# The first tap of the convolutions on ScalarE, and the low parts of their weights on VectorE instead of GpSimd

## The chip, the core and the metric

The kernel runs on one core of a Trainium2 chip. The core has a matrix engine (TensorE, PE in the profile), an elementwise engine (VectorE, DVE), an engine for activation functions and scaled copies (ScalarE, ACT), a general engine (GpSimd, POOL) and SyncE (SP), which here only issues DMAs. Each engine takes its own instructions strictly in order, and waits on semaphores for the others. The metric is the device time of one execution in microseconds; lower is better.

## The reference, cut to what matters

The reference is one step of a small diffusion backbone with 128 context and 512 latent tokens of width 1024: a mixer (neighbourhood attention and a gated DeltaNet in both directions) followed by an MLP. All of it is in float32. The part around the change projects the normalised tokens to the 1536 DeltaNet channels, convolves every channel along the tokens with five taps (context and latent tokens apart, each with zero padding), and applies silu:

```python
p = h @ w_in
dn_qkv = jax.nn.silu(_dwconv(dn_qkv, conv_w))      # CONV_W = 5, one filter per channel
dq, dk, dv = jnp.split(dn_qkv, [DN_QK_WIDTH, 2 * DN_QK_WIDTH], axis=-1)
dq = _l2n(dq.reshape(B, T, DN_HEADS, DN_DK))
dk = _l2n(dk.reshape(B, T, DN_HEADS, DN_DK))
```

What follows the projection (the DeltaNet, the attention, the merge and the MLP) takes most of the time and is not touched.

## The kernel before

TensorE multiplies float32 numbers as two rounded parts. Every operand is split into a high part (a cast to the rounded type) and a low part (the operand minus its high part), and a product is three matmuls: high with high, high with low, low with high. The helper `split` (lines 176 to 184) does it for a weight block of 128 x 1024 numbers: ScalarE makes the high part at line 182, and the engine named by `eng` makes the low part at line 183. `load_w` is a load through SyncE (line 174) and a split. The low part is formed by VectorE unless the call says otherwise; the call for the convolution's blocks says GpSimd. Four buffers each hold high and low parts.

The tokens (640 columns) stay in `hhi` and `hlo`, made in a front stage in which TensorE, VectorE, ScalarE and SyncE follow an order written out by hand. There VectorE forms a scaled copy `hf` (line 382) and the low part of one slice of the tokens (line 385) for TensorE's products at line 391; first VectorE has to form the modulation factors (line 247 and 250) from which ScalarE makes the high part.

Then come the twelve weight blocks of the DeltaNet channels, in three groups of four (q, k, v). For each block TensorE makes two products of 320 columns into two of two PSUM banks (lines 202 to 204, 48 matmuls). ScalarE copies them into a padded row buffer `cvb` (lines 624, 625, 626; there are two such buffers), which frees the banks. The five taps are one scaled copy and four multiply-adds on 128 x 644 numbers, all on VectorE:

```python
y = cb.tile([P, 644], F32, tag="y", name="y", bufs=2)
V.tensor_scalar(y, b[:, 0:644], cw[:, mt * 5 : mt * 5 + 1], None, op0=ALU.mult)   # line 628
for j in range(1, 5):
    V.scalar_tensor_tensor(y, b[:, j : j + 644], cw[:, mt * 5 + j : mt * 5 + j + 1], y,
                           op0=ALU.mult, op1=ALU.add)                             # line 630
```

Silu is a tanh on ScalarE (line 633) and a multiply-add on VectorE (line 634), which writes the block's channels. In the q group ScalarE also squares them (line 637) and TensorE sums the squares (line 639). In the k and v groups TensorE transposes the finished channels (line 643) once per block; ScalarE copies and squares the k results (lines 651, 653) and VectorE scales the v results (line 647), which are stored through ScalarE's DMA queue.

Beside the blocks run small chains: the z products (ScalarE 502, VectorE 503, GpSimd 504 and a store), the decay rates (VectorE 532 to 552, ending in `gg`, which TensorE reads at line 558), the norms of q and k (VectorE 149 to 158) and some factors that GpSimd forms and index rows that it loads (lines 662 to 680, 768, 769). The first weight blocks of the stage behind are cast by ScalarE at line 1055 and get their low parts from VectorE at line 1059.

Outside the hand-ordered stages a planner sets each engine's order before the run. It plays the program with its own costs and lets an engine take the ready instruction that stands first in the program. So the order around the twelve blocks is the planner's, and it follows which engine each instruction is given to. The front stage before and the stages behind the first two units of the next projection are ordered by hand.

Of the kernel before, what the change touches and what calls it, by code (L numbers as in the profile page):

```python
# [13 lines left out]
AF = mybir.ActivationFunctionType  # L14
ALU = mybir.AluOpType
# [5 lines left out]
KT = 8  # L21
# [76 lines left out]
def body(ctx: ExitStack, tc: tile.TileContext, I, O, dbg=None):  # L98
    nc = tc.nc
    dbg = dbg or {}  # L100
    V, S, G, PE = nc.vector, nc.scalar, nc.gpsimd, nc.tensor
# [9 lines left out]
    def ps_mm():  # L111
        return pp.tile([P, 512], F32, tag="mm", name="ps_mm", bufs=2)
# [4 lines left out]
    def ps_tb():  # L117
        return pp.tile([P, 512], F32, tag="tb", name="ps_tb", bufs=1)
# [3 lines left out]
    def ps_t3():  # L122
        tcnt[0] += 1
        return ps_tp() if tcnt[0] % 3 else ps_tb()

    def ps_st(i):
        return pp.tile([P, 512], F32, tag=f"st{i}", name=f"ps_st{i}", bufs=1)
# [18 lines left out]
    def newton_rsqrt(pool, x, n, tag, w=None, post=1.0, between=()):  # L146

        y, t, i = [pool.tile([P, w or n], ty, tag=tag + a, name=tag + a)[:, :n] for a, ty in (("y", F32), ("t", F32), ("i", I32))]
        V.tensor_scalar(i, x.bitcast(I32), 1, None, op0=ALU.logical_shift_right)
        V.tensor_scalar(y.bitcast(I32), i, -1.0, float(0x5F3759DF), op0=ALU.mult, op1=ALU.add)  # L150
        for it in range(3):
            V.scalar_tensor_tensor(t, y, -0.5, y, op0=ALU.mult, op1=ALU.mult)
            V.tensor_tensor(t, t, x, op=ALU.mult)
            if it < len(between):
                between[it]()
            V.scalar_tensor_tensor(y, t, 1.5, y, op0=ALU.add, op1=ALU.mult)
        if post != 1.0:
            V.tensor_scalar(y, y, post, None, op0=ALU.mult)
        return y
# [6 lines left out]
    def load_raw(src, pool=None, tag="raw"):  # L166
        if raw3[0] and tag == "raw":
            raw3[1] += 1
            if raw3[1] % 3 == 0:
                pool, tag = (raw3[0], 1), "raw3"  # L170
        pool = pool or (rawp if tag == "raw" else (wpool, 4))
        raw = pool[0].tile([P, 1024], F32, tag=tag, name="raw", bufs=pool[1])
        with tc.issue_after(behind[0]) if behind else ExitStack():
            lastd[0] = nc.sync.dma_start(raw, src).ins
        return raw

    def split(raw, kt, n, pool=None, eng=V):

        pool = pool or wpool
        hi = pool.tile([P, 1024], F32R, tag="whi", name="whi")  # L180
        lo = pool.tile([P, 1024], F32R, tag="wlo", name="wlo")
        S.copy(hi, raw)  # L182
        eng.tensor_tensor(lo, raw, hi.bitcast(F32), op=ALU.subtract)  # L183
        return [x.rearrange("p (k n) -> p k n", k=kt) for x in (hi, lo)]

    def load_w(src, kt, n, pool=None, eng=V):
        return split(load_raw(src), kt, n, pool, eng)
# [10 lines left out]
    def mm3(out, pairs):  # L198

        n = len(pairs)  # L200
        for i, (ah, al, bh, bl) in enumerate(pairs):
            PE.matmul(out, ah, bh, start=(i == 0), stop=False)  # L202
            PE.matmul(out, ah, bl, start=False, stop=False)  # L203
            PE.matmul(out, al, bh, start=False, stop=(i == n - 1))  # L204
# [97 lines left out]
    cw = cv.tile([P, 60], F32, tag="cw", name="cw")  # L302
# [186 lines left out]
    def feat_pairs(whi, wlo, half):  # L489
        a, w = HALVES[half]  # L490
        return [(whi[:, k], wlo[:, k], hhi[:, k, a : a + w], hlo[:, k, a : a + w]) for k in range(KT)]
# [122 lines left out]
    for x in range(3):  # L614
        sT = (kqS[:, 1], kqS[:, 0], vT)[x]
        pss = ps_tb() if x == 0 else None
        for hp in range(HP):
            mt = 4 * x + hp
            whi, wlo = load_w(I["w_dn"][mt], KT, 128, eng=G)
            ps0, ps1 = ps_mm(), ps_mm()  # L620
            mm3(ps0[:, :320], feat_pairs(whi, wlo, 0))
            mm3(ps1[:, :320], feat_pairs(whi, wlo, 1))
            b = cvb[mt % 2]
            S.copy(b[:, 2:130], ps0[:, 0:128])
            S.copy(b[:, 134:326], ps0[:, 128:320])
            S.copy(b[:, 326:646], ps1[:, :320])  # L626
            y = cb.tile([P, 644], F32, tag="y", name="y", bufs=2)
            V.tensor_scalar(y, b[:, 0:644], cw[:, mt * 5 : mt * 5 + 1], None, op0=ALU.mult)
            for j in range(1, 5):
                V.scalar_tensor_tensor(y, b[:, j : j + 644], cw[:, mt * 5 + j : mt * 5 + j + 1], y,  # L630
                                       op0=ALU.mult, op1=ALU.add)
            ty = cb.tile([P, 644], F32, tag="ty", name="ty", bufs=1)
            S.activation(ty, y, AF.Tanh, scale=0.5)
            V.scalar_tensor_tensor(sT[:, hp], ty, 1.0, y, op0=ALU.add, op1=ALU.mult)
            if x == 0:
                s2 = cb.tile([P, 644], F32, tag="s2", name="s2", bufs=2)
                S.activation(s2, sT[:, hp], AF.Square)
                for t in range(5):
                    PE.matmul(pss[:, 8 * t + 2 * hp : 8 * t + 2 * hp + 2], s2[:, TS[t] : TS[t] + 128], halves2, start=True, stop=True)
        for t in range(5) if x else ():  # L640
            ps = ps_t3() if x == 1 else ps_st(t % 3)
            for hp in range(HP):
                PE.transpose(ps[:, hp * 128 : hp * 128 + 128], sT[:, hp, TS[t] : TS[t] + 128], ident)
            if x == 2:
                for d in range(2):
                    vs = cb.tile([P, 644], F32, tag=("s2", "y")[d], name="vs", bufs=2)[:, :512]
                    V.tensor_tensor(vs.rearrange("p (h d) -> p h d", h=8), ps.rearrange("p (h d) -> p h d", h=8),
                                    vsc[:, d, t].unsqueeze(2).to_broadcast([P, 8, 64]), op=ALU.mult)
                    nc.scalar.dma_start(vs_d[d, t], vs)
            else:  # L650
                S.copy(kt[:, t], ps)
                s2 = cb.tile([P, 644], F32, tag="s2", name="s2", bufs=2)[:, :512]
                S.activation(s2, ps, AF.Square)
                V.tensor_reduce(ss[:, t], s2.rearrange("p (h d) -> p h d", h=8), axis=AX.X, op=ALU.add)
        if x < 2:

            s4 = cb.tile([P, 40], F32, tag="s4", name="s4")
            V.tensor_scalar(s4, ss.rearrange("p t h -> p (t h)") if x else pss[:, :40], 4 * EPS, None, op0=ALU.add)
            rs = newton_rsqrt(cb, s4, 40, "l2", post=(0.0625 if x == 0 else 1.0)).rearrange("p (t h) -> p t h", t=5)
            if x == 0:  # L660
                for y in (SF, SB):
                    G.tensor_copy(y[:, :, 4], rs)
                continue

            bb = bp.rearrange("p t (e h) -> p e t h", e=2)
            for d in range(2):
                G.tensor_tensor(bb[:, d], beta[:, :, 8 * d : 8 * d + 8], rs, op=ALU.mult)

            V.tensor_scalar(vsc[:, 1], bb[:, 1], 0.5, None, op0=ALU.mult)
            V.scalar_tensor_tensor(vsc[:, 0], s4.rearrange("p (t h) -> p t h", t=5), 0.5, rs, op0=ALU.mult, op1=ALU.mult)  # L670
            for d in range(2):
                G.tensor_tensor(bb[:, d], bb[:, d], rs, op=ALU.mult)
            G.tensor_copy(SF[:, :, 0], bb[:, 0])
            G.tensor_tensor(SF[:, :, 1], bb[:, 0], E4[:, 1], op=ALU.mult)
            G.tensor_tensor(SB[:, :, 2], bb[:, 1], E4[:, 2], op=ALU.mult)
            for par in range(2):
                sl = slice(64 * par, 64 * par + 64)
                G.tensor_copy(SX[sl, par : par + 9 : 2], SF[sl])
                G.tensor_copy(SX[sl, 1 - par], SB[sl, 0])
                G.tensor_copy(SX[sl, 3 - par : 10 - par : 2][:, ::-1], SB[sl, 1:5])  # L680

            V.scalar_tensor_tensor(rq2, SX[:, :, 4], 4.0 / 64, SX[:, :, 4], op0=ALU.mult, op1=ALU.mult)
# [666 lines left out]
    with (  # L1349
# [161 lines left out]
        with tc.manual_schedule(engines={E_.PE, E_.DVE, E_.Activation, E_.SP}):  # L1511
            late[0] = 1
            rot, oraw, subs = rotations(1, xq), [], []
            for j in range(-2, n + 1):
                hp, b = BLK[min(j + 2, n - 1)]
# [77 lines left out]
    for c in range(4):  # L1593
        whi, wlo = wbr[c]
# [429 lines left out]
    with tc.tile_pool(name="fin", bufs=2, side="right", reuse_waits="tile") as fin_:  # L2024
        gB2 = gate_bcast(1, fin_)
        w = {(kh, nh): split(w2_raw(7, kh, nh), 2, 512) for nh in range(2) for kh in range(2)}
        for blk in (None, (0, 0), (1, 0), (0, 1), (1, 1)):
            r = 0 if blk is None else 1
            if blk is None:
                parts = [(slice(0, 128), 0, slice(0, 128))]  # L2030
                y = [R[4][:, n] for n in range(2)]
                lhs = [[x[:, k] for x in fpr] for k in range(4)]
            else:
                th, pair = blk
                parts = [(slice(64 * j, 64 * j + 64), 1 + 2 * pair + j, slice(64 * th, 64 * th + 64)) for j in range(2)]
                y = [R[2 * th + n][:, pair] for n in range(2)]
# [122 lines left out]
```

## Time and profile before

| | |
|---|---|
| median of 3 runs | 1105.38 us (1104.59 to 1108.61) |
| the profiled execution | 1109.01 us, its span 1107.2 us |
| mean granted TensorE clock of the profiled execution | 0.99 |
| busy share of the span: PE, DVE, ACT, POOL | 96%, 77%, 47%, 28% |
| stretch of the twelve blocks | about 70 to 187 us of the span |

Rows of the timeline give the start and the length in microseconds, the engine, the line, the operation, what it writes and reads, and in brackets how long the engine stood idle before and who ended that. Rows of groups give the count, the busy time, the mean of one in ns, and the idle time before. Rows of waits give the total, the number of waits and the longest. A window's row gives, for each engine, busy time and instructions, and then the granted clock of TensorE as a share of full speed, the DMA engines' busy share and GB/s.

### The profile page before, as it was taken

The page shows a single profiled execution, that of the slowest core. Times are in us where ns is not written, and L with a number is a line of the kernel's source. Part 1 is how long each engine was busy: PE and PEld are TensorE (multiplying, and loading weights), DVE is VectorE, ACT ScalarE, POOL GpSimd, SP SyncE. Part 2 cuts the span into 40 slices and gives each one's busy share as a digit, 9 for nine tenths or more (in the row PEclk, how much of TensorE's full clock was granted, in tenths as well). Part 3 has the DMA queues.
Part 4 walks back from the last instruction along what each step waited for, and adds up shares of the span by engine and source line. Part 5 has one row for each costly group of instructions (what it writes and reads, how often), then busy time and mean ns, then how long its engine had stood idle before and what let it go on. Part 6 is the DMA issues. An engine that isn't in the chain of part 4 may idle for free.

```text
span 1107.2 us, 25427 instructions
## 1 busy us (share of the span) xinstructions
PE 1058.1 (96%) x10323; PEld 945.8 (85%) x10323; DVE 847.4 (77%) x1645; ACT 520.7 (47%) x1142; POOL 308.6 (28%) x276
## 2 busy tenths in 40 slices
PE   6999999999998998999999999999999999999996
PEld 5778989988888897888888999988888979797975
DVE  5557888497687677576857676999798887979775
ACT  5535443434353643336764442765444444444432
POOL 0242312000000001202504235335344352535213
PEclk9999999989999999999999999999999999999999
DMA  9832113564665655657537542465656556545605
GB/s 340 293 124 62 27 32 106 188 233 167 184 189 169 206 169 175 170 157 228 164 95 261 203 165 97 94 173 152 156 150 167 170 140 167 151 135 152 191 20 152
DMA packets 71972, 176.43 MB, mean 159 GB/s; under 512 B 18936, under 2 KB 28408, under 8 KB 71856
## 3 DMA queue, kind: packets, MB, share of 16 engines
q1 hardware_dynamic: 55504, 135.40, 36.5%
q0 software_dynamic: 9808, 24.80, 11.0%
q10 hardware_dynamic: 6544, 14.61, 4.0%
q8 instruction: 81, 1.33, 0.5%
q14 instruction: 35, 0.29, 0.1%
HBM read 150.62 MB, written 24.12 MB: 158 GB/s over the span
## 4 chain that ended last, share of the span: by engine, by line
PE 71%; DVE 19%; ACT 3%; issue 3%; DMA 2%; POOL 0%; DVEq 0%; ACTq 0%
PE ps_mm L1116 6%; PE ps_mm L1118 5%; PE ps_mm L1117 5%; DVE wlo L183 4%; PE ps_mm L1759 3%; PE ps_mm L1758 3%; PE ps_mm L1757 3%; PE ps_mm L202 3%; PE ps_mm L203 2%; PE ps_mm L204 2%; DVE R L1870 2%; DVE y L630 2%; PE ps_st L1759 2%; PE ps_st L1758 2%; PE ps_st L1757 2%
## 5 line engine op out<-in xcount | busy, mean ns | idle before, releaser
L1116 PE MATMUL ps_mm<-hhi,whi 128*128 128x320 f32 x384 | 130.3, 339 | 0.9 <-ACT gth L1072 0.9
L1118 PE MATMUL ps_mm<-hhi,wlo 128*128 128x320 f32 x384 | 120.6, 314 | 1.5 <-issue 1.5
L1117 PE MATMUL ps_mm<-hlo,whi 128*128 128x320 f32 x384 | 120.4, 314 | 0.0
L183 DVE TENSOR_TENSOR wlo<-raw,whi 128x1024 fp32r<-128x1024 f32 x59 | 81.3, 1386 | 21.5 <-ACT whi L182 21.2
L182 ACT CAST whi<-raw 128x1024 fp32r<-128x1024 f32 x78 | 81.0, 1046 | 31.1 <-PE ps_mm L1758 8.5
L1116 PEld LDWEIGHTS ps_mm<-hhi,whi 128*128 128x128 f32 x384 | 74.0, 193 | 10.2 <-issue 6.2
L1117 PEld LDWEIGHTS ps_mm<-hlo,whi 128*128 128x128 f32 x384 | 74.3, 194 | 0.2
L1118 PEld LDWEIGHTS ps_mm<-hhi,wlo 128*128 128x128 f32 x384 | 74.0, 193 | 0.0
L183 POOL TENSOR_TENSOR wlo<-raw,whi 128x1024 fp32r<-128x1024 f32 x19 | 46.5, 2449 | 72.4 <-ACT whi L182 72.4
L202 PE MATMUL ps_mm<-hhi,whi 128*128 128x320 f32 x192 | 60.8, 317 | 1.5 <-ACT cvb L626 1.5
L203 PE MATMUL ps_mm<-hlo,whi 128*128 128x320 f32 x192 | 60.6, 315 | 0.0
L204 PE MATMUL ps_mm<-hhi,wlo 128*128 128x320 f32 x192 | 60.1, 313 | 0.0
L183 DVE TENSOR_TENSOR wlo<-S,whi 128x1024 fp32r<-128x1024 f32 x28 | 54.8, 1973 | 4.2 <-ACT whi L182 4.2
L1359 POOL DMA_DIRECT2D vw<-v_d x32 | 21.1, 674 | 130.3 <-ACT arow L1133 93.2
L183 DVE TENSOR_TENSOR wlo<-T,whi 128x1024 fp32r<-128x1024 f32 x28 | 44.0, 1570 | 15.3 <-ACT whi L182 15.3
L768 POOL DMA_DIRECT2D rls<-ai_d x10 | 5.1, 509 | 174.7 <-PE ps_tb L731 161.8
L1059 DVE TENSOR_TENSOR wlo<-raw,whi 128x1024 fp32r<-128x1024 f32 x35 | 42.7, 1223 | 12.5 <-ACT whi L1055 12.1
L182 ACT CAST whi<-T 128x1024 fp32r<-128x1024 f32 x28 | 29.4, 1050 | 34.2 <-PE ps_mm L1758 16.5
L630 DVE SCALAR_TENSOR_TENSOR y<-cvb,cw,y 128x644 f32<-128x644 f32 x48 | 42.6, 888 | 0.9
L182 ACT CAST whi<-S 128x1024 fp32r<-128x1024 f32 x28 | 28.8, 1051 | 23.9 <-PE ps_tb L204 12.3
L1055 ACT CAST whi<-raw 128x1024 fp32r<-128x1024 f32 x35 | 36.5, 1047 | 7.0 <-issue 6.1
L1072 ACT ACTIVATE gth<-ps_mm 128x320 f32<-128x320 f32 x32 | 14.0, 437 | 53.5 <-PE ps_mm L1131 30.3
(579 smaller groups left out, 3549.1 us busy)
## 6 DMA issues: line engine op xcount, KB each, us to landing
raw<-in_w_ff_dram SPq DMA_DIRECT2D x57, 512.0 KB
raw<-in_w_ada_dram SPq DMA_DIRECT2D x48, 512.0 KB
raw<-in_w_gate_dram SPq DMA_DIRECT2D x16, 512.0 KB
S<-in_w_ff_dram SPq DMA_DIRECT2D x14, 512.0 KB
T<-in_w_ff_dram SPq DMA_DIRECT2D x14, 512.0 KB
S<-in_w_ff_dram POOLq DMA_DIRECT2D x14, 512.0 KB, 5.4
T<-in_w_ff_dram POOLq DMA_DIRECT2D x14, 512.0 KB, 7.1
raw<-in_w_dn_dram SPq DMA_DIRECT2D x12, 512.0 KB
```

Source lines behind the costliest of these rows:

```text
L182: S.copy(hi, raw)
L183: eng.tensor_tensor(lo, raw, hi.bitcast(F32), op=ALU.subtract)
L202: PE.matmul(out, ah, bh, start=(i == 0), stop=False)
L203: PE.matmul(out, ah, bl, start=False, stop=False)
L204: PE.matmul(out, al, bh, start=False, stop=(i == n - 1))
L630: V.scalar_tensor_tensor(y, b[:, j : j + 644], cw[:, mt * 5 + j : mt * 5 + j + 1], y, op0=ALU.mult, op1=ALU.add)
L1116: PE.matmul(ps, ah, bh, start=(k == 0), stop=False)
L1117: PE.matmul(ps, ah, bl, start=False, stop=False)
L1118: PE.matmul(ps, al, bh, start=False, stop=(k == KT - 1))
L1757: PE.matmul(o, hi[:, k, fs], bh, start=(first and k == 0), stop=False, skip_group_check=not first)
L1758: PE.matmul(o, hi[:, k, fs], bl, start=False, stop=False, skip_group_check=not first)
L1759: PE.matmul(o, lo[:, k, fs], bh, start=False, stop=(k == 3), skip_group_check=not first)
```

## The change

Two instructions of the loop over the twelve blocks change their engine. The low part of a block's weights is formed by VectorE, the default of the helper, and not by GpSimd. The first tap is an activation on ScalarE that copies the row buffer with a scale per channel, and not a multiplication on VectorE. The results are the same numbers. Nothing else of the program's text changes; the planner orders the stretch anew.

```diff
-            whi, wlo = load_w(I["w_dn"][mt], KT, 128, eng=G)
+            whi, wlo = load_w(I["w_dn"][mt], KT, 128)
             ps0, ps1 = ps_mm(), ps_mm()
             mm3(ps0[:, :320], feat_pairs(whi, wlo, 0))
...
             y = cb.tile([P, 644], F32, tag="y", name="y", bufs=2)
-            V.tensor_scalar(y, b[:, 0:644], cw[:, mt * 5 : mt * 5 + 1], None, op0=ALU.mult)
+            S.activation(y, b[:, 0:644], AF.Copy, scale=cw[:, mt * 5 : mt * 5 + 1])
             for j in range(1, 5):
```

## The prediction

> **What bounds the kernel now.** I read the busy shares first.
>
> ```profile
> PE 1058.1 (96%) x10323; PEld 945.8 (85%) x10323; DVE 847.4 (77%) x1645; ACT 520.7 (47%) x1142; POOL 308.6 (28%) x276
> ```
>
> TensorE (PE) is busy nearly throughout, so the time can only fall where TensorE stands still or runs at a lower clock. The second view is TensorE's waits between 40 and 200 us, the stretch in which the twelve weight blocks are prepared and convolved.
>
> ```profile
> PE ps_tp L643 <- DVE kqS L634: 2.6, 3, 1.5
> PE ps_mm L202 <- ACT cvb L626: 1.5, 1, 1.5
> PE ps_st L391 <- DVE hlo L385: 1.2, 1, 1.2
> PE ps_tp L558 <- DVE gg L552: 1.0, 1, 1.0
> ```
>
> Together 6.3 us in six waits. The columns are the total, the number of waits and the longest. The profile models a matmul's end about 0.16 us later than the next one starts in a dense stream (0.31 us long, 0.147 us apart), so the true standstill may be 6 x 0.16 = 1.0 us more: 7.3 us.
>
> The third view, the windows, shows the clock and the load around them.
>
> ```profile
> core 0: us, PE busy (x) PEld busy (x) DVE busy (x) ACT busy (x) POOL busy (x), PEclk, DMA share, GB/s
> 90.00:96.00 6.00, 4.84 (x35) 4.76 (x36) 5.89 (x7) 1.42 (x5) 3.59 (x5) 0.95 0.29 91
> 96.00:102.00 6.00, 6.00 (x35) 4.81 (x33) 1.82 (x3) 4.72 (x19) 0.73 (x1) 0.76 0.00 0
> 138.00:144.00 6.00, 4.74 (x32) 4.66 (x33) 5.09 (x5) 1.99 (x5) 2.39 (x1) 1.00 0.00 0
> 162.00:168.00 6.00, 6.00 (x43) 6.00 (x42) 6.00 (x10) 3.95 (x10) 0.00 (x0) 1.00 0.24 87
> ```
>
> Right after the two waits near 90 us the granted clock drops: 6 x (1 - 0.95) + 6 x (1 - 0.76) = 1.74 us of TensorE time are lost there.
>
> Now the cause of the waits. The timeline shows one turn of the loop over the blocks, for the k channels:
>
> ```profile
> 145.90 0.74 ACT L633 ACTIVATE ty<-y 128x644 f32<-128x644 f32 x1 [5.91 <-DVE y L630]
> 146.54 1.03 ACT L182 CAST whi<-raw 128x1024 fp32r<-128x1024 f32 x1
> 146.67 0.83 DVE L634 SCALAR_TENSOR_TENSOR kqS<-ty,y 128x644 f32<-128x644 f32 x1 [0.87 <-ACT ty L633]
> 147.48 0.42 ACT L626 COPY cvb<-ps_mm 128x320 f32<-128x320 f32 x1
> 147.56 0.44 PE L643 MATMUL ps_tp<-cst,kqS 128*128 128x128 f32 x2 [0.59 <-DVE kqS L634]
> 147.65 2.38 POOL L183 TENSOR_TENSOR wlo<-raw,whi 128x1024 fp32r<-128x1024 f32 x1 [5.90 <-ACT whi L182]
> 147.80 0.27 ACT L624 COPY cvb<-ps_mm 128x128 f32<-128x128 f32 x1
> 147.93 2.46 DVE L628 TENSOR_SCALAR y<-cvb,cw 128x644 f32<-128x644 f32 x1 [0.43 <-ACT cvb L626]
> 147.95 0.42 PE L202 MATMUL ps_mm<-hhi,whi 128*128 128x320 f32 x1
> 150.43 3.67 DVE L630 SCALAR_TENSOR_TENSOR y<-cvb,cw,y 128x644 f32<-128x644 f32 x4
> 154.19 0.74 ACT L633 ACTIVATE ty<-y 128x644 f32<-128x644 f32 x1 [5.90 <-DVE y L630]
> ```
>
> From tanh to tanh it takes 154.19 - 145.90 = 8.29 us: tanh, cast, copy L626 on ScalarE (ACT), first tap L628 and four further taps on VectorE (DVE), then the next tanh. TensorE's next product (147.95) starts as copy L626 frees its PSUM bank, and that copy stands behind the tanh in ScalarE's order. TensorE itself needs 8.29 - 0.59 = 7.70 us a turn. So the loop through ScalarE and VectorE is the longer one. Its odd member is L628, 2.46 us:
>
> ```profile
> L628 DVE TENSOR_SCALAR y<-cvb,cw x12: 544/576/3145, 83.8 to 178.5; 128x644 f32<-128x644 f32 x12
> 52.77 2.89 DVE L382 TENSOR_SCALAR hf<-kt,mod 128x128 f32<-128x128 f32 x2
> 55.29 2.61 POOL L183 TENSOR_TENSOR wlo<-raw,whi 128x1024 fp32r<-128x1024 f32 x1 [0.17 <-ACT whi L182]
> 55.76 2.82 DVE L385 TENSOR_TENSOR hlo<-hf,hhi 128x640 fp32r<-128x640 f32 x1
> 59.61 0.80 DVE L382 TENSOR_SCALAR hf<-kt,mod 128x128 f32<-128x128 f32 x2
> 60.51 0.82 DVE L385 TENSOR_TENSOR hlo<-hf,hhi 128x640 fp32r<-128x640 f32 x1
> 89.85 2.40 POOL L183 TENSOR_TENSOR wlo<-raw,whi 128x1024 fp32r<-128x1024 f32 x1 [7.60 <-ACT whi L182]
> 89.89 2.46 DVE L550 SCALAR_TENSOR_TENSOR po<-t,po 128x80 f32<-128x80 f32 x1
> ```
>
> Undisturbed, L628 takes 0.55 us (the minimum). It is long when it begins inside a GpSimd (POOL) subtraction, and it ends just after that ends (147.65 + 2.38 = 150.03; VectorE goes on at 150.43). The same befalls L385 (2.82 against 0.82 us) and L550: a VectorE instruction that meets a running subtraction of GpSimd waits for its end. All four kinds of wait hang on this. L385 is what TensorE waits for at 58.6 us; L550 is followed by gg L552, awaited by L558; the tanh chain holds L626 at 89.7 us and L634 from 137 us on.
>
> ```profile
> 88.10 0.74 ACT L633 ACTIVATE ty<-y 128x644 f32<-128x644 f32 x1 [5.92 <-DVE y L630]
> 89.68 0.42 ACT L626 COPY cvb<-ps_mm 128x320 f32<-128x320 f32 x1
> 90.15 0.41 PE L202 MATMUL ps_mm<-hhi,whi 128*128 128x320 f32 x1 [1.46 <-ACT cvb L626]
> 92.73 0.23 DVE L552 SCALAR_TENSOR_TENSOR gg<-po,ab 128x80 f32<-128x80 f32 x1
> 93.02 0.75 PE L558 MATMUL ps_tp<-gg,cst 128*128 128x40 f32 x5 [1.00 <-DVE gg L552]
> ```
>
> **The change part by part.** The prices, from the groups between 60 and 190 us (count, busy us, mean ns):
>
> ```profile
> L183 POOL TENSOR_TENSOR wlo<-raw,whi 128x1024 fp32r<-128x1024 f32 x9 | 21.6, 2399 | 27.4 <-ACT whi L182 27.4
> L628 DVE TENSOR_SCALAR y<-cvb,cw 128x644 f32<-128x644 f32 x12 | 17.3, 1442 | 4.9 <-ACT cvb L626 4.9
> L633 ACT ACTIVATE ty<-y 128x644 f32<-128x644 f32 x12 | 8.9, 742 | 36.4 <-DVE y L630 35.6 <-DVE l2y L150 0.8
> L1059 DVE TENSOR_TENSOR wlo<-raw,whi 128x1024 fp32r<-128x1024 f32 x5 | 6.2, 1245 | 0.3
> L788 ACT ACTIVATE DB<-Dm,bp 128x64 f32<-128x64 f32 x8 | 2.0, 342 | 0.0
> ```
>
> - *First tap to ScalarE.* VectorE loses 12 instructions, 17.3 us. ScalarE gains 12 of 128x644. The tanh of that shape costs 0.742 us, which is the lower bound; the new one also reads a scale per partition, as L788 does, whose whole 64-column instruction is 0.342 us, so 0.742 + 0.342 = 1.08 us is the upper bound. I take 0.83, nearer the tanh, as most of L788 is not the pointer. That is 12 x 0.83 = 10 us on ScalarE, hidden while ScalarE idles (busy 1.99 of 6 us at 138:144); without that cover up to 10 us would show. Behind it in ScalarE's order stand the next block's copies L624, L625, which then free their bank 0.8 us later; TensorE needs that bank half a turn (3.8 us) later.
>   The Trainium skill, "ScalarE: Activation LUTs" (What ACT_TABLE_LOAD costs), puts a per-partition pointer operand at about 93 ns; by it the tap is an estimated 0.742 + 0.093 = 0.835 us. No row here separates that.
> - *Subtraction to VectorE.* GpSimd loses 12 subtractions, 9 after 60 us (21.6 us) and three before. VectorE gains 12; the same shape costs it 1.245 us in L1059 where GpSimd is quiet, and, if it meets another GpSimd job as long as the present ones, 1.245 + 2.399 = 3.6 us. I take 1.245, the nearest row, since the twelve long jobs are the ones removed: 9 x 1.245 = 11.2 us against 17.3 us removed, so VectorE has less to do. The first three fall beside the hand-ordered front, where L385 gives back 2.82 - 0.82 = 2.0 us and the pair L382 2.89 - 0.80 = 2.1 us, while three subtractions cost 3.7. No DMA is added or moved; GpSimd's own later work (the z products, the index loads) only gets an emptier queue, SyncE's queue is unchanged. The low parts have four buffers and feed products up to three blocks later, so a late one has up to 3 x 7.7 = 23 us of cover.
> - *The loop afterwards.* Tanh at 0, cast from 0.64 to 1.67, copy L626 at 1.58, tap from 1.90 to 2.73 (147.80 - 145.90 = 1.90, then 0.83), the taps L630 and the hand-over 154.19 - 150.43 = 3.76: 6.5 us. VectorE's new subtraction needs the cast: from 1.67 to 2.92, so L630 starts at 2.92, not 2.73: 6.7 us. Should the planner put the subtraction ahead of product L634, add about 0.75: 7.4 us. With the 1.08 us tap and no subtraction in the way it is 6.7 us as well. All are under TensorE's 7.70, so TensorE bounds the turn and the waits on L643 and L202 go. L385 and gg are no longer held, so 1.2 and 1.0 us go too.
>
> What is late next is TensorE's own stream. The sum: waits -6.3 us (bounds: -7.3 with the modelled ends; -3.7 if the L643 waits stay); the clock dip, between 0 and -1.74, taken at half, -0.9; one new or remaining wait of the size seen in the loop, +0.6 (bounds 0 and the rivals below). Total -6.6 us. The stage behind (162:168) has TensorE full, so an earlier start is carried to the end.
>
> The profile's execution took 1109.0 us around its span of 1107.2, 3.6 us above the median of the three runs shown, 1105.38. So 1102.4 for the profiled one, and 1105.4 - 6.6 = 1098.8 us as a median.
>
> On the dip: the trace has PEclk 0.95 and 0.76 behind waits of 1.46 and 1.00 us and tiny products. The Trainium skill, "TensorE: Matmul & The Clock Gate" (Part 1), says the clock halves after an idle window of about 3.4 us on a free-running counter; by that rule removing these two waits removes the dip only if the tiny products fill the window, -1.74 or 0. The trace has a dip without 3.4 us of standstill, so I stay at half.
>
> **The rivals.**
> - *Part of it.* The planner's order keeps the transposes L643 early in TensorE's in-order stream, and they wait for L634 whatever the loop's length. For it: three waits of that kind, and the order is fixed before the run. Against: L634 would come some 1.6 us earlier in a turn (8.29 to 6.7). 6.3 - 2.6 = 3.7 us gained: 1101.7.
> - *Given back.* After 156 us VectorE is full (6.00 of 6 at 162:168), and it may hand the transposes of v over no earlier than now. Against: TensorE is full there too without a wait, and VectorE's net load falls by 17.3 - 11.2 = 6.1 us. Only L385's 1.2 us would be kept: about 1104.2.
> - *Slower: VectorE's strict order as a trap.* If the subtraction stands before L634, and on ScalarE the square L637, which needs L634, before L626, then: subtraction to 2.92, L634 to 3.7, square 0.74 to 4.4, L626 and 0.32 to 4.8, tap to 5.6, L630 and hand-over 3.76: 9.3 us a turn, 1.6 over TensorE's 7.70. It decides from 7.70 + 6.3/12 = 8.2 us a turn. Over twelve turns 19 - 6.3 = +13 us: 1118. Over the four q blocks alone, where the square is, it merely cancels the gain. For it: today cast and tanh already stand before L626. Against: today the square stands behind L626 at 90 us.
> - *No effect on VectorE's blocking* (GpSimd's other work blocks as much): nine of these long GpSimd jobs in this stretch are the subtractions, 21.6 us. It would give 1105, and its chance is counted with the case given back.
>
> **How the numbers follow.** Full effect 0.55 (own range 1096 to 1099.9), part of it 0.27 (1100 to 1104), given back or no effect 0.10 (1104 to 1107), slower 0.08. Half a per cent is 5.5 us, about what can be told from no change. Faster by more: 0.55; within: 0.37; slower: 0.08. The range: low end 6.3 + 1.0 + 1.74 = 9.0 us gained plus 0.6 of spread, 1095.8; high end in the given-back case, 1106.
>
> **What would show it.** Right: no VectorE instruction of this stretch over 2 us; the new tap on ScalarE 0.74 to 0.9 us; VectorE's subtraction about 1.25 us; a turn of 7.4 to 7.7 us with TensorE's waits between 40 and 200 us under 1.5 us in sum; the end of v's taps some 6 us earlier. Wrong: waits of TensorE on L643 or L626 of the old size (part), waits at the transposes of v or in the hand-ordered stage after it (given back), or turns over 8.2 us with VectorE waiting for the cast (trap).

## The result, and the profile after

| | before | after |
|---|---|---|
| median | 1104.99 us (1103.99 to 1108.61, 4 runs) | 1096.16 us (1095.03 to 1097.76, 4 runs) |
| profiled execution, its span | 1109.01, 1107.2 us | 1095.1, 1093.3 us |

The ratio is 0.9911, with a 95% interval of 0.9885 to 0.9936. On the 1105.38 us given at first that is 0.9911 x 1105.38 = 1095.5 us: a gain of 9.8 us where 6.6 were predicted, and just outside the range, whose low end was 1095.8. The interval reaches from 1092.7 to 1098.3 us, and the two medians of the table are only 8.8 us apart, so the 0.3 us outside the range can't be told from noise; that the gain is larger than 6.6 us can. One execution of 2559 us, of the kernel below with the first three subtractions on GpSimd, was in a slow state and is in no ratio.

The first part of the page of after, the busy shares:

```profile
PE 1054.6 (96%) x10323; PEld 944.4 (86%) x10323; DVE 834.6 (76%) x1645; ACT 530.8 (49%) x1154; POOL 278.7 (25%) x264
```

VectorE, which took over twelve subtractions and gave up twelve taps, is busy for 847.4 - 834.6 = 12.8 us less than before. Between 40 and 200 us its longest instruction takes 1.71 us; before, ten took over 2 us, up to 3.15. The view of TensorE's waits between 40 and 200 us, four rows and 6.3 us before, has no row left. The windows of after, at 90 and 96 us (the same windows as before):

```profile
90.00:96.00 6.00, 6.00 (x42) 5.10 (x41) 4.53 (x6) 3.83 (x16) 1.61 (x4) 1.00 0.27 90
96.00:102.00 6.00, 6.00 (x46) 5.43 (x45) 4.54 (x6) 5.97 (x13) 0.00 (x0) 1.00 0.33 99
```

TensorE is full and its clock is 1.00 in both windows that had 0.95 and 0.76. The groups of after between 40 and 190 us give the prices of the moved work:

```profile
L183 DVE TENSOR_TENSOR wlo<-raw,whi 128x1024 fp32r<-128x1024 f32 x12 | 15.1, 1264 | 4.9 <-ACT whi L182 4.6
L628 ACT ACTIVATE y<-cvb,cw 128x644 f32<-128x644 f32 x12 | 10.1, 841 | 0.2
L630 DVE SCALAR_TENSOR_TENSOR y<-cvb,cw,y 128x644 f32<-128x644 f32 x48 | 42.9, 893 | 3.0 <-ACT y L628 2.2
L385 DVE TENSOR_TENSOR hlo<-hf,hhi 128x640 fp32r<-128x640 f32 x4 | 3.3, 825 | 1.2 <-ACT hhi L376 0.9
```

The tap costs 0.841 us on ScalarE (taken: 0.83), the subtraction 1.264 us on VectorE (taken: 1.245). All four L385 now take 0.82 us, where one of them had taken 2.82. A turn of the loop in the timeline of after, ScalarE's and VectorE's rows that matter:

```profile
134.09 0.74 ACT L633 ACTIVATE ty<-y 128x644 f32<-128x644 f32 x1 [1.87 <-DVE y L630]
134.87 0.83 DVE L634 SCALAR_TENSOR_TENSOR kqS<-ty,y 128x644 f32<-128x644 f32 x1 [0.81 <-ACT ty L633]
...
135.76 1.05 ACT L182 CAST whi<-raw 128x1024 fp32r<-128x1024 f32 x1 [0.92 <-PE ps_mm L203]
...
136.84 1.23 DVE L183 TENSOR_TENSOR wlo<-raw,whi 128x1024 fp32r<-128x1024 f32 x1 [1.14 <-ACT whi L182]
137.16 0.84 ACT L628 ACTIVATE y<-cvb,cw 128x644 f32<-128x644 f32 x1
138.03 3.67 DVE L630 SCALAR_TENSOR_TENSOR y<-cvb,cw,y 128x644 f32<-128x644 f32 x4
...
141.74 0.74 ACT L633 ACTIVATE ty<-y 128x644 f32<-128x644 f32 x1 [1.82 <-DVE y L630]
```

From tanh to tanh it is 141.74 - 134.09 = 7.65 us, TensorE's own 7.70 within the spread, and the direction of waiting has turned round: ScalarE's cast waits for TensorE (the row at 135.76), and the tanh for 1.8 us where it was 5.9. One turn is not all: the eleven turns last 6.4 to 12.9 us before and 5.6 to 11.8 us after. The first and the last of the twelve tanh, before and after, give their sum:

```profile
L633 ACT ACTIVATE ty<-y x12: 723/742/755, 88.1 to 183.6; 128x644 f32<-128x644 f32 x12
```

```profile
L633 ACT ACTIVATE ty<-y x12: 722/744/810, 86.2 to 173.7; 128x644 f32<-128x644 f32 x12
```

The eleven turns take 183.6 - 88.1 = 95.5 us before and 173.7 - 86.2 = 87.5 us after, 8.0 us less.

The time is not all gained in this stretch. TensorE's first product of three stages marks the borders: L391 of the hand-ordered front, L1131 of the stage behind the blocks, L1103 of the stage after that. The lines of before (min/median/max in ns, first and last start in us):

```profile
L391 PE MATMUL ps_st<-whi,hhi x24: 389/393/502, 19.4 to 63.2; 128*128 128x512 f32 x24
L1131 PE MATMUL ps_mm<-raw,csl x512: 272/273/298, 224.3 to 453.9; 128*32 128x128 f32 x171
L1103 PE MATMUL ps_mm<-doh,wlo x64: 274/310/346, 526.2 to 588.5; 128*128 128x384 f32 x32, 128*128 128x256 f32 x32
```

and of after:

```profile
L391 PE MATMUL ps_st<-whi,hhi x24: 389/393/502, 18.3 to 62.7; 128*128 128x512 f32 x24
L1131 PE MATMUL ps_mm<-raw,csl x512: 272/273/297, 215.1 to 441.5; 128*32 128x128 f32 x171
L1103 PE MATMUL ps_mm<-doh,wlo x64: 274/311/346, 512.9 to 575.3; 128*128 128x384 f32 x32, 128*128 128x256 f32 x32
```

From L391 to L1131, the changed stretch: 204.9 before, 196.8 after, 8.1 us less. From L1131 to L1103, which the change does not touch (TensorE's products there are the same, and in the same order up to some thirty near the end): 301.9 and 297.8, 4.1 us less. The rest of the 13.9 us between the two spans is 1.1 us at the start (19.4 against 18.3) and 0.6 us behind. In the untouched stage the waits that the profile calls "issue" (TensorE waits for nothing that it shows) differ; before, between 200 and 540 us:

```profile
PE ps_tb L818 <- issue: 2.9, 1, 2.9
PE ps_mm L1118 <- issue: 1.5, 1, 1.5
PE ps_tp L826 <- issue: 1.3, 1, 1.3
PE ps_st L942 <- issue: 1.1, 1, 1.1
PE ps_st L921 <- issue: 0.7, 1, 0.7
```

and after:

```profile
PE ps_st L942 <- issue: 1.8, 1, 1.8
PE ps_tb L818 <- issue: 1.5, 1, 1.5
PE ps_mm L1117 <- issue: 0.7, 1, 0.7
```

7.7 us before (with one wait of 0.2 that is not shown) against 4.0 us.

### The profile page after: what moved, and what is told of

It reads as the page before. It is cut to its first block, busy times and chain, and to the rows that moved or that the text cites. A ratio compares the mean times of both kernels' runs of the same rounds, so it can differ in the third digit from the quotient of the medians.

```text
span 1093.3 us, 25408 instructions
## 1 busy us (share of the span) xinstructions
PE 1054.6 (96%) x10323; PEld 944.4 (86%) x10323; DVE 834.6 (76%) x1645; ACT 530.8 (49%) x1154; POOL 278.7 (25%) x264
## 3 DMA queue, kind: packets, MB, share of 16 engines
q8 instruction: 81, 1.33, 0.5%
## 4 chain that ended last, share of the span: by engine, by line
PE 79%; DVE 14%; ACT 3%; issue 2%; DMA 2%; SPq 0%; DVEq 0%; ACTq 0%
PE ps_mm L1116 6%; PE ps_mm L1117 5%; PE ps_mm L1118 5%; PE ps_mm L202 4%; PE ps_mm L203 4%; PE ps_mm L204 4%; DVE wlo L183 4%; PE ps_mm L1759 3%; PE ps_mm L1758 3%; PE ps_mm L1757 3%; DVE R L1870 2%; PE ps_st L1759 2%; PE ps_st L1758 2%; PE ps_st L1757 2%; PE ps_st L391 2%
## 5 line engine op out<-in xcount | busy, mean ns | idle before, releaser
L183 DVE TENSOR_TENSOR wlo<-raw,whi 128x1024 fp32r<-128x1024 f32 x71 | 96.7, 1369 | 26.3 <-ACT whi L182 25.7
L1059 DVE TENSOR_TENSOR wlo<-raw,whi 128x1024 fp32r<-128x1024 f32 x35 | 42.7, 1222 | 15.6 <-ACT whi L1055 13.7
L630 DVE SCALAR_TENSOR_TENSOR y<-cvb,cw,y 128x644 f32<-128x644 f32 x48 | 42.9, 893 | 3.0 <-ACT y L628 2.2
L1759 PE MATMUL ps_mm<-mhi,wlo 128*128 128x320 f32 x112 | 34.0, 314 | 4.3 <-DVE wlo L183 4.3
```

Of the source, the lines that this page charges most:

```text
L1759: PE.matmul(o, lo[:, k, fs], bh, start=False, stop=(k == 3), skip_group_check=not first)
```

## The experiments

The theory, A in the expectations: a running GpSimd subtraction holds VectorE's instructions until it ends, this made the loop longer than TensorE's turn, and moving the subtraction is what gains; the tap's move adds little. Its rivals are that the tap's move gains (VectorE's load), that the planner's new order gains, and that part of the gain is chance between executions. F is a theory on the issue waits, formed after the first runs. Ratios are against the kernel before, run beside each on the same chip (medians of 1105.9, 1106.4 and 1105.3 us). The table collects, from each kernel's profile, the stretch from L391 to L1131, TensorE's waits in it (40 to 200 us), the TensorE time lost to a lower granted clock (window length times one minus the clock, summed over windows of 6 us from 18 to 222 us), the stage from L1131 to L1103, the issue waits between 200 and 540 us, and the TensorE time lost to the clock in that stage (windows of 6 us from 228 to 528 us). All but the ratios are in us.

| kernel | ratio (95%) | stretch | waits | clock lost | stage behind | issue | clock lost behind |
|---|---|---|---|---|---|---|---|
| before | 1 | 204.9 | 6.3 | 1.74 | 301.9 | 7.7 | 6.84 |
| before again | 1.0002 (0.9982 to 1.0022) | 205.2 | 6.4 | 1.68 | 302.7 | 8.1 | 5.10 |
| after | 0.9911 (0.9885 to 0.9936) | 196.8 | 0 | 0 | 297.8 | 4.0 | 6.78 |
| after again | 0.9910 (0.9890 to 0.9930) | 196.7 | 0.2 | 0 | 297.9 | 4.4 | 6.84 |
| subtraction only | 0.9913 (0.9891 to 0.9935) | 195.8 | 0 | 0 | 298.3 | 5.9 | 5.10 |
| tap only | 0.9976 (0.9956 to 0.9995) | 203.0 | 2.9 | 3.42 | 299.0 | 4.4 | 5.04 |
| after, extra GpSimd work | 1.0008 (0.9985 to 1.0030) | 206.4 | 3.9 | 5.16 | 307.6 | 10.1 | 10.20 |
| after, extra VectorE work | 0.9921 (0.9903 to 0.9939) | 196.8 | 0.3 | 0 | 301.7 | 6.3 | 6.78 |
| after, first three on GpSimd | 0.9916 (0.9892 to 0.9939) | 197.6 | 1.3 | 1.68 | 297.6 | 5.4 | 5.10 |
| after, seven more moved | 0.9940 (0.9920 to 0.9959) | 198.2 | 0 | 3.36 | 298.0 | 4.4 | 5.16 |
| after, 32 more transposes | 0.9974 (0.9949 to 0.9999) | 199.0 | 0.3 | 1.68 | 294.3 | 3.8 | 1.74 |
| after, 64 more transposes | 0.9922 (0.9895 to 0.9949) | 196.7 | 0 | 0 | 300.2 | 6.4 | 5.10 |

The stage behind is 294.3 to 307.6 us long. Less its issue waits and its lost clock it is 286.7 to 289.6 us in all twelve profiles, so these two make most of its differences. Between the first profiles of before and after it is the issue waits, 3.7 us less, with the same lost clock. Between the second ones the issue waits are 3.7 us less too, but the lost clock is 1.74 us more, so that 2.8 of the 4.8 us are neither.

The mean granted clock of each timed execution is on record as well. Its span times one minus that clock is the TensorE time that it lost; the averages are 10.0 us before (59 executions), 8.5 after (10), 8.2 with the subtraction alone (6), 11.8 with the tap alone (12) and 12.4 with the extra GpSimd work (12). By these figures about 1.4 us of the gain are clock, hardly more than the scatter of the averages (about 0.9).

**The kernel before, unchanged.**

> The kernel before once more, against itself. Both theories: ratio 1.000 within 0.003. Its second profile shows how much the waits that the profile calls issue, behind 200 us, differ from execution to execution (7.7 us in the first profile of before, 4.0 in that of after): if by some 4 us, the part of the 13.9 us between the two profiled spans that arose behind 267 us is no effect of the change.

The waits of TensorE between 40 and 200 us in this second execution:

```profile
PE ps_tp L643 <- DVE kqS L634: 2.7, 3, 1.5
PE ps_st L391 <- DVE hlo L385: 1.4, 1, 1.4
PE ps_mm L202 <- ACT cvb L626: 1.3, 1, 1.3
PE ps_tp L558 <- DVE gg L552: 1.0, 1, 1.0
```

and its windows in the front and where the clock had dropped before:

```profile
18.00:24.00 6.00, 5.46 (x31) 4.38 (x28) 5.18 (x17) 2.52 (x7) 0.00 (x0) 0.72 1.03 410
90.00:96.00 6.00, 4.34 (x33) 4.26 (x34) 5.89 (x8) 1.94 (x6) 3.37 (x4) 1.00 0.27 91
96.00:102.00 6.00, 6.00 (x43) 5.07 (x43) 2.36 (x4) 4.77 (x19) 1.15 (x3) 1.00 0.00 0
```

The same four waits come back to 0.2 us: they belong to the kernel. The clock dip near 90 us does not come back, but there is one of the same size in the front, and the stretch is as long (205.2 against 204.9 us). So the place of a dip is a matter of the execution, and these two profiles don't show what it costs. The issue waits of the stage behind came back at 8.1 us, so the difference there is hardly chance between the two first profiles.

**The subtraction alone.** The tap stays on VectorE.

```diff
-            whi, wlo = load_w(I["w_dn"][mt], KT, 128, eng=G)
+            whi, wlo = load_w(I["w_dn"][mt], KT, 128)
```

> Only the twelve subtractions go to VectorE; the first tap stays on VectorE. Theory A (a VectorE instruction waits for a running GpSimd subtraction, and that lengthens the loop): the tap takes 0.55 us everywhere, a turn takes 2.92 + 0.55 + 3.76 = 7.2 us, under TensorE's 7.70, all six waits of TensorE go, gain 7 to 9 us, ratio 0.992 to 0.994. Theory B (VectorE has too much work, and moving the tap is what helps): VectorE loses only the blocking, a turn is near 8 us, gain at most 3 us, ratio 0.997 or more.

The whole gain, ratio 0.9913. The tap's group in it:

```profile
L628 DVE TENSOR_SCALAR y<-cvb,cw x12: 548/550/553, 82.8 to 169.5; 128x644 f32<-128x644 f32 x12
```

Before, the same instruction on the same engine took 544 to 3145 ns; without a GpSimd subtraction under it, it takes 0.55 us twelve times out of twelve. The planner's order differs from that of after (another product stands at 387 of the 10323 places in TensorE's order, as TensorE's small products lie elsewhere among the blocks), and the time doesn't.

**The tap alone.** The subtraction stays on GpSimd.

```diff
-            V.tensor_scalar(y, b[:, 0:644], cw[:, mt * 5 : mt * 5 + 1], None, op0=ALU.mult)
+            S.activation(y, b[:, 0:644], AF.Copy, scale=cw[:, mt * 5 : mt * 5 + 1])
```

> Only the first tap goes to ScalarE; GpSimd keeps the twelve subtractions. Theory A: the next tap L630, which also reads two arrays of SBUF, meets the running subtraction in the place of the first and takes 2 us and more, a turn stays at 8.0 to 8.4 us, the waits on L385 (1.2 us) and gg (1.0 us) stay, gain 0 to 2 us, ratio 0.998 to 1.000. Theory B: gain 4 to 8 us, ratio 0.993 to 0.996.

2.7 us faster by the ratio, 0.9976, a little more than the theory had. A turn in its timeline:

```profile
143.72 0.74 ACT L633 ACTIVATE ty<-y 128x644 f32<-128x644 f32 x1 [4.41 <-DVE y L630]
...
145.47 2.39 POOL L183 TENSOR_TENSOR wlo<-raw,whi 128x1024 fp32r<-128x1024 f32 x1 [5.25 <-ACT whi L182]
...
146.62 4.70 DVE L630 SCALAR_TENSOR_TENSOR y<-cvb,cw,y 128x644 f32<-128x644 f32 x4 [1.30 <-ACT y L628]
...
151.35 0.74 ACT L633 ACTIVATE ty<-y 128x644 f32<-128x644 f32 x1 [4.39 <-DVE y L630]
```

The four taps take 4.70 us in place of 3.67: the first of them is now the one that is held, until 145.47 + 2.39 = 147.86. But ScalarE's tap has run beside the same GpSimd job, so a block loses some 1.0 us to it and not 2.46 - 0.55 = 1.9, and this turn is 7.63 us, TensorE's, where 8.0 to 8.4 were expected. The waits on L643 are gone with it; those of the small chains are not (L391 still has its 1.3 us), and the clock falls right behind that of L558:

```profile
PE ps_tp L558 <- DVE gg L552: 1.6, 1, 1.6
```

```profile
90.00:96.00 6.00, 5.74 (x30) 5.74 (x31) 4.29 (x6) 3.26 (x19) 4.21 (x5) 0.63 0.30 91
96.00:102.00 6.00, 6.00 (x34) 4.42 (x33) 1.65 (x2) 4.18 (x7) 0.00 (x0) 0.80 0.02 3
```

In this profile the lost clock seems to count in full: the stretch is 203.0 - 196.8 = 6.2 us longer than after's, and the waits and the lost clock make 2.9 + 3.42 = 6.3.

**After, with the GpSimd work put back as work of no use.** For blocks 3 to 11 GpSimd forms the same difference into a scratch tile that nobody reads; VectorE forms the real one. Below it the line numbers are 4 higher.

```diff
-            whi, wlo = load_w(I["w_dn"][mt], KT, 128)
+            raw_ = load_raw(I["w_dn"][mt])
+            whi, wlo = split(raw_, KT, 128)
+            if mt >= 3:
+                scr = cb.tile([P, 1024], F32R, tag="scr", name="scr")
+                G.tensor_tensor(scr, raw_, whi.rearrange("p k n -> p (k n)").bitcast(F32), op=ALU.subtract)
```

> The changed kernel, to which GpSimd's subtraction is added again for blocks 3 to 11, from the same inputs into a buffer that nobody reads (work added, the outputs unchanged). Theory A: VectorE meets it again, a turn goes to 8 us or more where it lands on the chain, TensorE's waits come back, the gain shrinks to 4 us or less (ratio 0.996 or more). Theory C (the planner's other order of the stretch brings the gain, not the end of the blocking): the ratio stays at 0.991 to 0.993, since only GpSimd's queue is changed.

The gain is gone, ratio 1.0008. Its groups between 60 and 200 us:

```profile
L634 DVE SCALAR_TENSOR_TENSOR y<-cvb,cw,y 128x644 f32<-128x644 f32 x48 | 48.8, 1016 | 2.9 <-ACT y L632 2.2
L623 POOL TENSOR_TENSOR scr<-raw,whi 128x1024 fp32r<-128x1024 f32 x9 | 27.1, 3016 | 31.3 <-issue 17.8 <-ACT whi L182 13.5
```

The 48 taps take 48.8 us, against 42.9 in after. TensorE's waits between 40 and 200 us are on the same chains as before, and in the windows the clock falls behind that of L558:

```profile
PE ps_tp L647 <- DVE kqS L638: 1.8, 2, 1.0
PE ps_tp L558 <- DVE gg L552: 1.6, 1, 1.6
PE ps_mm L202 <- ACT cvb L630: 0.5, 1, 0.5
```

```profile
90.00:96.00 6.00, 6.00 (x27) 5.82 (x26) 5.36 (x5) 3.58 (x19) 5.18 (x5) 0.50 0.21 60
```

The stretch is 206.4 - 196.8 = 9.6 us longer than after's; waits and lost clock make 3.9 + 5.16 = 9.1. More than half of it is the clock, in this one execution. It is the slowest of the twelve timed, 1114.5 us, and its stage behind is 9.8 us longer as well, so it is luck that the median's loss, 9.8 us, has the size of the stretch's. By the clock on record the twelve executions lost 12.4 us to it on average, and those with the subtraction alone, of the same session, 8.2. So some 4 us of the loss are clock, which comes back in this experiment together with the waits. Theory C falls: TensorE's order is that of after but for 17 of the 10323 places, and the gain is gone.

**After, with the same extra work on VectorE.** `G.tensor_tensor` of the last diff becomes `V.tensor_tensor`; nothing else.

> The changed kernel, to which the subtraction of blocks 3 to 11 is added a second time, on VectorE, into a buffer that nobody reads (the same added work as with GpSimd, on the other engine; outputs unchanged). Theory A: 1.23 us more on VectorE make a turn of 6.7 + 1.2 = 7.9 us, hardly over TensorE's 7.70; 0 to 3 us lost, ratio 0.991 to 0.994. Rival (the stretch has no room for nine more such jobs wherever they are): the gain is lost as with GpSimd's, ratio 0.998 or more.

```profile
L623 DVE TENSOR_TENSOR scr<-raw,whi 128x1024 fp32r<-128x1024 f32 x9 | 12.0, 1337 | 0.0
```

Ratio 0.9921, 1.1 us above after (1096.41 in the same session), a difference within the intervals, and a stretch as long as after's. So 12 us more on VectorE cost next to nothing, and 27 us on GpSimd, which stands idle between these jobs, cost everything. That decides against the load of VectorE as the cause.

**After, with the first three blocks' subtraction on GpSimd**, the ones beside the hand-ordered front:

```diff
-            whi, wlo = load_w(I["w_dn"][mt], KT, 128)
+            whi, wlo = load_w(I["w_dn"][mt], KT, 128, eng=G if mt < 3 else V)
```

> The changed kernel with the first three of the twelve subtractions back on GpSimd. Theory A: only the three jobs beside the front are long again, L385 and L382 take 2.8 us, TensorE waits for L385 1.2 to 1.4 us and for nothing else in the stretch, 1 to 2 us of the gain are lost (ratio 0.992 to 0.9935). Rival: the front has slack behind it (filler products), and nothing is lost (ratio as the changed kernel's of the same chip).

The wait of L391 on L385 comes back alone, 1.3 us, and the stretch is 0.8 us longer than after's. In the time (0.9916 against 0.9910) it can't be told. Its profile also lost 1.68 us to a clock dip in the front, so the 0.8 us can't be put down to that wait alone. The front's part of the gain is shown by the wait only.

**After, unchanged**, beside the last two:

> The changed kernel once more. Ratio 0.989 to 0.9935. Its second profile: up to 267 us the gain of the stretch should be about 8 us again. For the hand-ordered stage behind (from the first L942 to the first L1103 with doh and wlo; 259.0 and 259.9 us in two profiles of before, 254.8 in that of after): theory N, its length varies from execution to execution, so it lies anywhere from 254 to 260; theory F, it goes with the program (the place of its instructions), so it is 255 again.

0.9910, with the stretch and the stage behind within 0.1 us of the first profile of after; from the first L942 it is 513.8 - 258.6 = 255.2 us, as theory F had it and theory N allowed. Both executions of before have 302 to 303 us in the stage behind and 8 us of issue waits, both of after 298 and 4.

**After, with seven more low parts moved in the MLP.** Near the end of the kernel one more split forms its low parts on GpSimd:

```diff
-        prompt(1, split(B12, 2, 512, eng=G), b22)
+        prompt(1, split(B12, 2, 512), b22)
```

> The changed kernel, and beside it the one remaining call that gives a low part to GpSimd (seven weight blocks of the MLP stage) also goes to VectorE. Theory A: the seven jobs of 2.4 us no longer hold VectorE there (its longest subtraction is 2.9 us against 1.22), TensorE's waits on the low parts (L1759, 4.3 us in six) shrink, 1 to 4 us more are gained: ratio 0.987 to 0.990. Rival: VectorE is busy 80 to 90% there and 7 x 1.25 = 8.7 us more work lengthens the waits: ratio 0.992 to 0.997.

Not faster: 0.9940 (0.9920 to 0.9959), at the median 2.3 us above after's 1096.41. TensorE's waits for VectorE's low parts there, in this kernel and then in after:

```profile
PE ps_mm L1759 <- DVE wlo L183: 4.8, 6, 1.4
```

```profile
PE ps_mm L1759 <- DVE wlo L183: 4.3, 6, 1.2
```

In that stage TensorE waits for low parts that VectorE formed already, and the seven moved ones queue among them. But that does not make the kernel slower either: from the first L1103 to the end of the span it is 1095.9 - 516.0 = 579.9 us here and 1093.3 - 512.9 = 580.4 in after. Theory A missed here: those waits did not shrink. What is longer in this profile is the stretch of the blocks, by 1.4 us, in which it lost 3.36 us in two clock dips, far ahead of the edit. By the clock on record the six executions lost 10.4 us on average and those of after in the same session 7.7, which is about the size of the 2.3 us of the median. So this move gains nothing that can be told, and whether it costs anything is open (the two intervals touch).

**After, with 32 and with 64 more transposes ahead of everything.** The issue waits remained. Theory F says that TensorE waits for a block of its instruction stream, so that such a wait sits at a fixed place of the stream, and moves by as many products as are put ahead. The added transposes write a bank that nobody reads. The diff is of the first; the second has 98.

```diff
-            for i in range(34):
+            for i in range(66):
                 PE.transpose(warm[:, i % 4 * 128 : i % 4 * 128 + 128], ident, ident)
```

> The changed kernel with 32 more warm-up transposes at its very start (66 for 34; their results are never used). They cost 1 to 4 us at the start and shift every later TensorE instruction by 64 places in its stream. Theory F (behind 200 us TensorE now and then waits for its next block of instructions, at places fixed in the stream, and the changed kernel's shorter hand-ordered stage comes from where these fall): the issue waits between 200 and 540 us move to other matmuls and their sum leaves 4.0 to 4.6 us by 1 us or more; the stretch between matmul 1380 and matmul 6800 (counted without the added ones; 306.1 and 306.2 us in two profiles of the changed kernel, 310.2 and 311.0 in two of before) changes with it. Theory G (these waits hang on how full the DMA queues are then, and not on the place): the stretch stays 306 us and the waits keep their matmuls.

> The same with 64 more (98 for 34), a shift of 128 instructions. Theory F: the places of the waits move once more, the sum of the issue waits differs from both others. Theory G: as in the changed kernel, 4 to 5 us at the same matmuls.

The largest two rows of issue waits with 32 more:

```profile
PE ps_mm L1131 <- issue: 1.7, 2, 1.1
PE ps_tp L826 <- issue: 1.4, 1, 1.4
```

The wait that stood before the 2884th product (counted through the trace) now stands before the 2852nd and, with 64 more, before the 2820th, counted without the added ones: moved by 32 and 64. Others moved with it or vanished; that of L818 is in neither. The places are as F has them. Its forecast that the sum of the issue waits leaves 4.0 to 4.6 us by 1 us came with 64 more (6.4) and missed with 32 more (3.8). Nor do places explain before: between before and after they differ by one product (2885 and 2884, 3648 and 3647), and before's waits are longer. The price is not settled: with 32 more the profiled execution has a stage of 294.3 us, with the least issue waits and lost clock of all, but it is the fastest of the ten, 1096.2 us, and the median is 1102.2 us (0.9974, 0.9949 to 0.9999); with 64 more the median is 1098.4 us (0.9922, 0.9895 to 0.9949), and the profile has 300.2 and 6.4.

## Where the prediction was right, and which step failed

- *The cause was right, and shown.* VectorE's instructions were held by running GpSimd subtractions, and this made the loop the longer one. Put the work back on GpSimd and the gain goes (1.0008), give the same work to VectorE and it stays (0.9921). The Trainium skill, "SBUF — State Buffer" (SBUF: two separate sides), describes it as a port pair that one engine locks for a whole instruction while the other blocks entirely; the traces agree, with L628 at 2.46 us over a subtraction and 0.55 without, and an L385 at 2.82 and 0.82.
- *The two edits were not priced apart*; the runs do it. The subtraction alone has all of the gain. The tap alone gains 2.7 us, as 0.84 us of the chain then run beside the GpSimd job, and adds nothing that can be told once that job is gone.
- *The prices were right*: 0.841 against 0.83 us, 1.264 against 1.245, the turn shown 7.65 against "7.4 to 7.7". The estimate for the tap by the Trainium skill, "ScalarE: Activation LUTs" (What ACT_TABLE_LOAD costs), 0.835 us, agrees with 0.841 as well.
- *The waits were right*: 6.3 us, foretold under 1.5, measured 0 and 0.2.
- *The step that failed is in the sum: a term for a wait that did not come, and none for the stage behind.* The profiles have 204.9 - 196.8 = 8.1 us in the stretch where the sum had 6.6. Its term "one new or remaining wait of the size seen in the loop, +0.6" was wrong: the waits left are 0 and 0.2 us. Without it, with the dip counted in full, the sum is 6.3 + 1.74 = 8.0. That the dip counts in full is not shown. In the second execution of before, 8.4 us above after, waits and lost clock make 6.4 + 1.68 = 8.1; but the kernel with seven more moved lost 3.36 us of clock in a stretch only 1.4 us longer than after's. The timed executions have about 1.4 us less lost clock after the change, over the whole kernel, where half a dip, 0.9, was taken. The 1.0 us of modelled ends was left in the bound and not taken into the sum; no run prices it.
- *The stage behind had no term.* "An earlier start is carried to the end" was taken as all that could happen there. In the profiles this untouched stage is 4.1 and 4.8 us shorter, and the issue waits that it holds are 3.7 us shorter in both pairs of executions. Why they are shorter is not shown. But the stage does not follow the engine of the low parts: with the tap alone it is 299.0 us, with the extra VectorE work 301.7. The timed gain, 9.8 to 10.0 us with an interval of 7 to 13 in the first comparison, has room for about 1.5 us of it beside the 8.1 to 8.4 of the stretch, if the stretch of the profiles is the usual one. The low end, "9.0 us gained plus 0.6 of spread", left no room for a gain behind the stretch, and the time came out 0.3 us below it.
- *The rivals fell.* "Part of it": no L643 wait stayed. "Given back": v's taps end early and nothing takes it back; the last tanh, which follows them, starts 9.9 us earlier (183.6 and 173.7), where about 6 were expected; 1.1 us of these come from before the stretch. The trap: the subtraction stands behind L634 in the turn shown, 7.65 us. VectorE does wait for the cast, 4.6 us in all twelve blocks, and four of the eleven turns are over 8.2 us (before, eight), but TensorE waits in none of them. No effect: the twelve long jobs were what held VectorE in this stretch.

What stays open: how much of the issue waits there is in the executions of which no trace is kept, and so how the timed 9.8 us divide between the stretch, the stage behind and the clock. The profiled gain, 13.9 us, is larger than the timed one. No kernel of this study beats after; the one with the subtraction alone equals it.

## What to carry to other kernels

When one kind of VectorE instruction shows a minimum of 0.55 us and a maximum of 3.1, look for the GpSimd instruction that runs beneath the long ones: an elementwise job on an idle GpSimd can be paid for by VectorE (here L628 was held for up to 3.15 - 0.55 = 2.6 us, to save 1.25 of VectorE's own). It is worth moving where the held instruction lies on the loop that bounds, and the test is the turn of the loop against TensorE's own time. In a sum of waits, keep a term for what differs between executions (a clock dip, the instruction stream): here these were as large as the error of the sum.

## What the runs showed of the hardware that was not expected

- *Not every VectorE instruction is held.* In before, the GpSimd subtraction that starts at 69.29 us takes 2.36 us. L503, which reads one of its inputs from PSUM, runs inside it in 0.69 us (70.28 us), and so does L532 in 0.23 us (71.37 us). So the prediction's "a VectorE instruction that meets a running subtraction of GpSimd waits for its end" is too wide. What decides it was not tested here.
- *The clock falls by half for about 3.4 us or a multiple of it, behind short waits or none, and not at the same places in every execution.* In the stretch TensorE waited for at most 1.6 us at a time, and the granted clock went to 0.50 for a whole window of 6 us (90 to 96 us, extra GpSimd work). At half clock the 1.74, 3.42 and 5.16 us lost are dips of 3.5, 6.8 and 10.3 us, near 1, 2 and 3 times 3.4. Windows cut to the dip of the kernel with 32 more transposes show one such length:

```profile
90.50:92.10 1.60, 1.55 (x14) 1.28 (x13) 1.14 (x2) 1.60 (x9) 0.24 (x1) 1.00 0.00 0
92.20:95.50 3.30, 3.30 (x15) 2.52 (x15) 3.00 (x4) 1.18 (x9) 1.49 (x4) 0.50 0.45 155
95.70:97.00 1.30, 1.30 (x8) 0.82 (x7) 0.83 (x1) 1.25 (x4) 0.00 (x0) 1.00 0.00 0
```

  The Trainium skill, "TensorE: Matmul & The Clock Gate" (Part 1), has the clock decided by a free-running window of about 3.4 us; the lengths fit, but a standstill of 3.4 us is nowhere in the stretch. Near 90 us the place is that of the tiny products at L558. Of the four profiles with a wait there, three have a dip, of one to three such lengths; of the eight without that wait two have one, of a single length. So the wait makes the dip likelier and longer, as far as twelve profiles can say, and its absence does not rule it out. It is not the only place: each of the twelve profiles loses 1.7 to 10.2 us in the stage behind, and in each a dip begins within 5 us of the start of a wait of 2.4 us there (L818, for a VectorE result).
- *Waits of TensorE on its own instruction stream.* They are 0.2 to 3.3 us each, 4 to 10 us a profile between 200 and 540 us, at fixed places of the stream (two of them 128 products apart, that is 256 instructions with their weight loads). Of the 60 in the twelve profiles, 55 end 1.1 to 1.6 us after a packet of the instruction queue has landed; the other five, 0.2 us each, stand before L726 and do not move with the transposes. The row of that queue on the page (packets, MB, share of the span) gives 1.33 MB / 81 = 16 KB a packet:

```profile
q8 instruction: 81, 1.33, 0.5%
```

- *Unused work of 32 transposes ahead of the kernel* cost 5.8 us at the median (1102.2 us, with after at 1096.4 in another session; by the ratios 7.1 us), and twice as much of it 2.0 us (1.3), which is not clear of noise. That the block borders shift with it is shown. That this is what cost the time is not: the executions with 32 more also lost 10.5 us to the clock on average, against 8.5 in after, and the rest is open.
